# A streaming-encoder block on one core: c spread by a load, the opening's first step by parts, and gate B applied inside attention

## The chip, the core and the metric

The kernel runs on one core of a Trainium2 chip. A core has TensorE (PE in the profile, with its weight loads as PEld), VectorE (DVE), ScalarE (ACT), GpSimd (POOL) and SyncE (SP); each works through its own instructions in order, and semaphores hold an instruction until what it needs is there. DMAs are issued by SP and ACT as items of their instruction queues. Matrix products go from SBUF to PSUM, which has eight banks of 128 x 512 fp32. The metric is the device time of one execution in microseconds (us), lower is better.

## What is computed

One layer of an encoder block for 1024 tokens of width 1024 (16 heads of 64, FFN width 2816), in fp32:

```python
mod = silu(c) @ ada_w + ada_b
sh1, sc1, g1, sh2, sc2, g2 = split(mod, 6)
h = rmsnorm(x, ln1_g) * (1 + sc1) + sh1
q, k, v, cb, cc, cx, ga, gb = split(h @ w_in)          # conv B, C, x; gates A, B
q, k = rmsnorm(q), rmsnorm(k)                          # per head
y_a = stick_breaking_attention(q, k, v)                # strictly causal, scan over the keys
y_b = cb * causal_dwconv(cc * cx, conv_w)
merged = sigmoid(ga) * (y_a @ w_branch_a) + sigmoid(gb) * (y_b @ w_branch_b)
x = x + g1 * (merged @ w_out)
h = rmsnorm(x, ln2_g) * (1 + sc2) + sh2
x = x + g2 * ((silu(h @ w_ffn_gate) * (h @ w_ffn_up)) @ w_ffn_down)
```

## The kernel before

**Products.** Each fp32 operand is split in a high part (rounded to fp32r, tiles named `hi`, `whi`, `hh`, `yh`) and a low rest (`lo`, `wlo`, `hl`, `yl`); a product is three passes, hi by hi, hi by lo and lo by hi, added up in one PSUM bank. For most splits ACT makes the high part and DVE the rest.

**Stages.** (1) The opening, (2) a second pass over w_kv and the k part, (3) the gates and convolution inputs (Strassen products), which store sigmoid(ga) and sigmoid(gb) to DRAM as `d_sga` and `d_sgb`, (4) attention, (5) the merge, (6) the output projection, (7) the FFN. A planner (a simulated timeline) orders instructions on the engines by their priority; the opening's order is kept as written, and in attention so are all PE instructions and attention's own on DVE.

**The opening** multiplies x, not yet normed, so that PE can start early. `cab` is silu(c) on all partitions: one row of c (`crow`, 4 KB) is loaded on the ACT queue, two products with a row of ones (L326) spread it over 128 partitions, and two Silus (L327) write it. `mod_dot` (L237, DVE) takes a strip of the ada weights (`ld<-ada`) times `cab` and sums it into one column; `scale_sum` makes of it `a1`, the scale of 128 features. `raw_hi` (L263, ACT) and `raw_lo` (L267, DVE) write hi and lo of x times a1; `split_hi` (L217) and `split_lo` (L222) split the weights. `real` (L294) adds, for each of eight steps k over the features, three passes for each of NR = 6 token blocks into six banks `psr`: in every step MC = 2 blocks first, then the other four. `warm` runs NW = 4 fp32 products of nothing of use (two passes each, L329) ahead of the first real one. Behind the eight steps `tail` does two more token blocks with the same operands; `square` (L252, ACT) has meanwhile summed the squares of x (`ld<-x`), `finish_raw` scales the finished blocks and empties their banks (L310 on ACT for even ones, L308 on DVE for odd ones), and `bcast` (L258, PE) writes the norm factors into banks thus emptied (`rsp`), for the products that follow. The loads stand on SP in the order ada, x, w_kv, ada, x and so on.

**Attention** (L870 to L1100) goes head by head: scores on PE (L900, L901), exponentials on ACT (L902), a scan on DVE (L910), transposes on PE (L924), their splits (L927 on ACT, L928 on DVE) and products with v. The scores leave PE time; `fillers()` yields other products into it: first C times B (`cb_w`), then W_b (L1000 to L1002, through `mm_ch`), for 16 pairs of an output block m and a token half n. ACT copies each finished W_b product out of its bank (`mb`, L1042), and SP stores it to DRAM (`d_mb`).

**The merge** (L1129 to L1153) forms for each of the same 16 pairs the W_a product (24 passes), and joins the branches: SP loads `sa` (sigmoid of gate A, tag "sgi", two buffers, L1139), `mb` (three buffers, L1141) and `sb` (sigmoid of gate B, tag "yr", two buffers, L1143); POOL multiplies mb by sb (L1144); DVE multiplies the product by sa (L1147, this empties the PSUM bank) and adds mb (L1148); ACT and DVE split the sum (L1152, L1153). Near the end `preload_wo` (L1107, one raw buffer) loads the first weights of the output projection and splits them (L1111 on ACT, L1112 on DVE).

Of the kernel before, what the change touches and what calls it, by code (L numbers as in the profile page):

```python
# [9 lines left out]
F32 = mybir.dt.float32  # L10
F32R = mybir.dt.float32r
AF = mybir.ActivationFunctionType
ALU = mybir.AluOpType
# [4 lines left out]
P = 128  # L18
T = 1024
D = 1024  # L20
# [10 lines left out]
def block_kernel(tc, x, x_t, cols, ada_1, ada_2, ada_row, w_q, w_kv, w_cg, w_a, w_b, w_o, w_g, w_u, w_d, out):  # L31
    nc = tc.nc
# [7 lines left out]
    def nm(s):  # L40
        uid[0] += 1
        return f"{s}_{uid[0]}"
# [31 lines left out]
    d_sgb = drp.tile([KT, P, T], F32, name="d_sgb")  # L74
# [7 lines left out]
    d_h = [drp.tile([P, 4, 512], F32, name=f"d_h{e}") for e in range(2)]  # L82
# [5 lines left out]
    mk = const.tile([P, D], F32, name="mk")  # L88
# [12 lines left out]
    nhalf = const.tile([P, 8], F32, name="nhalf")  # L101
    nc.vector.memset(nhalf, -0.5)
    cst = const.tile([P, 98], F32, name="cst")
    nc.scalar.dma_start(cst, cols)
    ct, ln1, ln2 = cst[:, 0:8], cst[:, 8:16], cst[:, 16:24]
    acol = cst[:, 24:56].rearrange("p (m k) -> p m k", m=4)
    cw = cst[:, 56:80].rearrange("p (k t) -> p k t", k=8)
    qgc, kgc = cst[:, 80:81], cst[:, 81:82]
    gcol = cst[:, 82:98].rearrange("p (m k) -> p m k", m=2)
    nc.vector.tensor_scalar(out=qgc, in0=qgc, scalar1=0.125, scalar2=None, op0=ALU.mult)  # L110
    mod = const.tile([P, 4, 8], F32, name="mod")
    const.tile([P, PADL // 4], F32, name="padl")
    st.enter_context(tc.tile_pool(name="padr", bufs=1, side="right", reuse_waits="tile")).tile(
# [30 lines left out]
    def ps_pj():  # L144
        return pps.tile([P, 512], F32, tag="pj", bufs=6, name=nm("pj"))
# [26 lines left out]
    sp = s1.enter_context(tc.tile_pool(name="start", bufs=1, reuse_waits="tile"))  # L172
# [4 lines left out]
        return xts[:, k, ns]  # L177

    cab = sp.tile([P, D], F32, name="cab")
    crow = sp.tile([1, D], F32, name="crow")  # L180
    nc.scalar.dma_start(crow, ada_row[0:1, :])
    rs = sp.tile([P, T], F32, name="rs")
    hh = [big() for n in range(2)]
    hl = [big() for n in range(2)]
# [14 lines left out]
        ads[m, k] = load_ring(ada_1[k][:, m])  # L199

    wq = []
    NLD, MC, NW, KB = 5, 2, 4, 2

    def load_wq(qt):
        wp, bufs = wps
# [9 lines left out]
    def split_hi(k):  # L215
        cs = slice(k % 2 * 512, k % 2 * 512 + 512)
        nc.scalar.activation(wq[k // 2][0][:, cs], wraw[k // 2][:, cs], AF.Copy)  # L217

    def split_lo(k):
        cs = slice(k % 2 * 512, k % 2 * 512 + 512)  # L220
        hi, lo = wq[k // 2]
        nc.vector.tensor_tensor(out=lo[:, cs], in0=wraw[k // 2][:, cs], in1=hi[:, cs].bitcast(F32), op=ALU.subtract)  # L222
# [17 lines left out]
    def scale_sum(k):  # L240
        nc.vector.scalar_tensor_tensor(out=a1[:, k:k + 1], in0=mod_dot(1, k), scalar=acp[:, k:k + 1],
                                       in1=ln1[:, k:k + 1], op0=ALU.add, op1=ALU.mult)
# [53 lines left out]
    def real(pss, k, ts, w):  # L296
        for parts in ((0,), (1,), (2,)):
            for i in ts:
                mm_tok(pss[i], i, w, k, k + 1, parts)
# [21 lines left out]
    load_ada(1, 3)  # L321
    load_x(3)
    warm = ps_tr()
    for e in range(2):
        t = ps_pj()
        nc.tensor.matmul(t, mk[0:1, D - P:], crow[:, e * 512:e * 512 + 512], start=True, stop=True)  # L326
        nc.scalar.activation(cab[:, e * 512:e * 512 + 512], t, AF.Silu)  # L327
    for e in range(NW):
        nc.tensor.matmul(warm, ident, mk[:, 512:], start=True, stop=True)  # L329
    scale_sum(0)  # L330
    raw_hi(0)
    split_hi(0)
    scale_sum(1)
    split_lo(0)
    raw_lo(0)
    split_hi(1)
    NR = 6
    psr = [ps_pj() for i in range(NR)] + [ps_tr() for i in range(8 - NR)]
    for k in range(KT):
        real(psr, k, range(MC), wq)  # L340
        if k + 1 < KT:
            raw_hi(k + 1)
            split_lo(k + 1)
        if k + 2 < KT:
            scale_sum(k + 2)
            split_hi(k + 2)
        if k + 1 < KT:
            raw_lo(k + 1)
        real(psr, k, range(MC, NR), wq)
        if k + 4 < KT:  # L350
            load_ada(1, k + 4)
            load_x(k + 4)
        if k % 2 == 0 and k < 6:
            load_wq(k // 2 + 2)
        if k > 2:
            load_xq(k - 3)
        if k > 3:
            square(k - 4)
# [199 lines left out]
    for cc in (1, 2):  # L558
        w = wq[8:] if cc == 1 else [load_w(w_kv[3, j]) for j in range(4)]
        for i_, i in enumerate(range(8) if cc == 1 else (4, 5, 6, 7, 0, 1, 2, 3)):  # L560
# [12 lines left out]
            ps = ps_pj()  # L573
# [227 lines left out]
    sg_.close()  # L801
    ftx.close()
    split_at[:] = [gw]
    for e in range(2):
        nc.sync.dma_start((hh, hl)[e][1][:, :4].bitcast(F32), d_h[e])
    psA.close()


# [195 lines left out]
    def fillers():  # L1004
        cb_w = {}
        for m, n in [(m + d, n) for m in range(0, KT, 2) for n in range(2) for d in range(2)]:
            if n == 0:
                cb_w[m] = load_ch(w_cg[0, m])
            w = cb_w[m]
            y = fp.tile([P, 512], F32, tag="st", bufs=3, name=nm("cy"))  # L1010
            nc.sync.dma_start(y, d_y[m, :, n * 512:(n + 1) * 512])
            ps = ps_f()
            for kk in range(0, KT, KQ):
                if kk:
                    yield 0.65 * KQ
                mm_ch(ps, w, hh[n], hl[n], kk, kk + KQ)
            nc.vector.tensor_tensor(out=y, in0=ps, in1=y, op=ALU.mult)
            yh = fq.tile([P, 512], F32R, tag="ybh", bufs=2, name=nm("ybh"))
            yl = fq.tile([P, 512], F32R, tag="ybl", bufs=2, name=nm("ybl"))
            nc.scalar.activation(yh, y, AF.Copy)  # L1020
            nc.vector.tensor_tensor(out=yl, in0=y, in1=yh.bitcast(F32), op=ALU.subtract)
            nc.sync.dma_start(d_yb[0][n][:, m, :], yh.bitcast(F32))
            nc.sync.dma_start(d_yb[1][n][:, m, :], yl.bitcast(F32))
            yield 0.65 * KQ
        yh, yl = [], []
        for n in range(2):
            yh.append(big())
            yl.append(big())
            for k in range(0, KT, 2):
                nc.sync.dma_start(yh[n][:, k:k + 2].bitcast(F32), d_yb[0][n][:, k:k + 2])  # L1030
                nc.sync.dma_start(yl[n][:, k:k + 2].bitcast(F32), d_yb[1][n][:, k:k + 2])
        wb = {}
        for m, n in [(0, 0), (1, 0), (0, 1), (1, 1)] + [(m, n) for m in range(2, KT) for n in range(2)]:
            if n == 0:
                wb[m] = load_ch(w_b[m])
            ps = ps_f()
            for kk in range(0, KT, KQ):
                if kk:
                    yield 0.65 * KQ
                mm_ch(ps, wb[m], yh[n], yl[n], kk, kk + KQ)  # L1040
            mb = fp.tile([P, 512], F32, tag="st", bufs=3, name=nm("mb"))
            nc.scalar.activation(mb, ps, AF.Copy)  # L1042
            nc.sync.dma_start(d_mb[m, :, n * 512:(n + 1) * 512], mb)
            yield 0.65 * KQ

# [16 lines left out]
    with tc.high_priority():  # L1062
        for j in range(HEAD):
            next(fl)
            if j == 1:
                vl = load_vlast(0)
                turn_vlast(0, vl)
                att_load(0)
                load_v(0, 1)
                load_v(0, 0)  # L1070
    at_ = attention()
    flush, nfl = [0], 0
    pe, mine = len(nc.cur_bb.bb.instructions), set()
# [58 lines left out]
    for m, n in [(0, 0), (1, 0), (0, 1), (1, 1)] + [(m, n) for m in range(2, KT) for n in range(2)]:  # L1132
        if (m, n) == (KT - 2, 0):
            with tc.issue_after(last_m.ins):
                preload_wo()
        if n == 0:
            wa[m] = load_ch(w_a[m])
        sa = fp.tile([P, 512], F32, tag="sgi", bufs=2, name=nm("sgi"))
        nc.sync.dma_start(sa, d_sga[m, :, n * 512:(n + 1) * 512])  # L1139
        mb = fp.tile([P, 512], F32, tag="st", bufs=3, name=nm("mb"))  # L1140
        nc.sync.dma_start(mb, d_mb[m, :, n * 512:(n + 1) * 512])  # L1141
        sb = fp.tile([P, 512], F32, tag="yr", bufs=2, name=nm("sgb"))
        nc.sync.dma_start(sb, d_sgb[m, :, n * 512:(n + 1) * 512])  # L1143
        nc.gpsimd.tensor_tensor(out=mb, in0=mb, in1=sb, op=ALU.mult)  # L1144
        ps = ps_f()
        mm_ch(ps, wa[m], yah[n], yal[n])
        last_m = nc.vector.tensor_tensor(out=sa, in0=ps, in1=sa, op=ALU.mult)  # L1147
        nc.vector.tensor_tensor(out=sa, in0=sa, in1=mb, op=ALU.add)  # L1148
        if m == 0:
            mh[n] = big()  # L1150
            mlo[n] = big()
        nc.scalar.activation(mh[n][:, m, :], sa, AF.Copy)  # L1152
        nc.vector.tensor_tensor(out=mlo[n][:, m, :], in0=sa, in1=mh[n][:, m, :].bitcast(F32), op=ALU.subtract)  # L1153
# [110 lines left out]
    for ch in range(2):  # L1264
# [21 lines left out]
        for i in (0, 4, 1, 2, 3, 5, 6, 7) if ch else range(8):  # L1286
# [8 lines left out]
            ps = bank()  # L1295
# [396 lines left out]
```

## Time and profile before

| what | us |
|---|---|
| three runs, median (lowest, highest) | 1832.03 (1830.80, 1834.08) |
| the profiled execution | 1830.19 |
| its span in the profile | 1828.4 |
| PE busy in the span | 1795.6 |
| DVE, ACT, POOL busy | 1360.4, 815.2, 388.9 |
| 16 products mb by sb on POOL, together (mean of one) | 21.6 (1.353) |

Rows of the timeline give start (us from the start of the span), duration (with xN the duration of N in a run of them), engine, line, operation, output<-input, shapes, and in brackets how long the engine stood idle before it and what ended that. Rows of the waits of PE give total us, times, and the longest. Groups by line end with busy us and the mean ns of one, then the idle time before them. Rows of windows are a stretch of the span with the busy time of PE, PEld, DVE, ACT and POOL, the granted clock of PE (1.00 is full), the busy share of the DMA engines and their GB/s. Rows on DMA give the size and the time from issue to landing. Passes overlap in PE, so the distance of two starts tells more than one's duration.

### The profile page before, as it was taken

How to read it: one execution, taken by the hardware profiler on the slowest of the kernel's cores; microseconds unless marked ns; L12 is line 12 of the kernel's file. 1: busy time of each engine (PE TensorE's matmuls, PEld its weight loads, DVE VectorE, ACT ScalarE, POOL GpSimd, SP SyncE). 2: the span in 40 equal slices, each digit the busy share in tenths (PEclk: the TensorE clock that was granted, in tenths of full speed). 3: DMA queues.
4: the chain of work that ended last, by engine and by line, in shares of the span. 5: the costliest groups of instructions: out<-in, count | busy, mean ns of one | idle time of the engine just before them, and what ended most of it. 6: DMA issues, size and time to landing. Idle time of an engine off the chain costs nothing. (4 is left out here: it accounts for less than half of the span.)

```text
span 1828.4 us, 24603 instructions
## 1 busy us (share of the span) xinstructions
PE 1795.6 (98%) x8635; PEld 1490.9 (82%) x8635; DVE 1360.4 (74%) x1964; ACT 815.2 (45%) x1527; POOL 388.9 (21%) x293
## 2 busy tenths in 40 slices
PE   8999999999999899999999989999999999999999
PEld 6888877888778788888888868877888888878887
DVE  5876586778895699998886544689977878644766
ACT  5434364333433476777675221664444344322321
POOL 0024334633232000000000210114534544200000
PEclk9999999999999999999999999999999999999999
DMA  9479644223684977696544656424543444299776
GB/s 365 155 240 383 237 176 141 84 98 112 236 291 161 265 204 184 194 330 153 146 114 132 201 173 221 136 87 162 195 148 140 149 164 160 105 361 326 278 230 219
DMA packets 164960, 359.05 MB, mean 196 GB/s; under 512 B 15507, under 2 KB 60891, under 8 KB 163686
## 3 DMA queue, kind: packets, MB, share of 16 engines
q1 hardware_dynamic: 128300, 289.65, 48.2%
q10 hardware_dynamic: 35530, 64.16, 9.8%
q0 software_dynamic: 1008, 3.67, 0.5%
q8 instruction: 69, 1.13, 0.3%
q14 instruction: 53, 0.43, 0.1%
HBM read 246.80 MB, written 110.66 MB: 196 GB/s over the span
## 5 line engine op out<-in xcount | busy, mean ns | idle before, releaser
L910 DVE TENSOR_TENSOR_SCAN pt<-pt,mk 128x128 f32<-128x128 f32 (+7 forms) x128 | 172.5, 1347 | 3.7 <-ACT pt L902 3.7
L133 PE MATMUL e<-big,whi 128*128 128x512 f32 x352 | 137.3, 390 | 2.8 <-ACT c L1420 1.4
L135 PE MATMUL e<-big,wlo 128*128 128x512 f32 x352 | 137.0, 389 | 0.0
L134 PE MATMUL e<-big,whi 128*128 128x512 f32 x352 | 137.0, 389 | 0.0
L294 PE MATMUL pj<-whi,big 128*128 128x512 f32 x448 | 132.9, 393 | 0.0
L138 DVE TENSOR_TENSOR c<-e,c 128x512 f32<-128x512 f32 x138 | 92.8, 686 | 49.7 <-PE e L135 48.6
L133 PE MATMUL pj<-big,whi 128*128 128x512 f32 x320 | 125.3, 392 | 1.8 <-DVE c L138 1.8
L1144 POOL TENSOR_TENSOR mb<-mb,sgb 128x512 f32<-128x512 f32 x16 | 21.6, 1353 | 494.3 <-DMA mb<-d_mb 454.5
L135 PE MATMUL pj<-big,wlo 128*128 128x512 f32 x320 | 124.8, 390 | 0.0
L134 PE MATMUL pj<-big,whi 128*128 128x512 f32 x320 | 124.6, 389 | 0.0
L1520 PE MATMUL e<-whi,f 128*128 128x512 f32 (+1 forms) x319 | 121.8, 382 | 1.4 <-DMA f<-d_f 1.4
L1521 PE MATMUL e<-wlo,f 128*128 128x512 f32 (+1 forms) x319 | 121.8, 382 | 0.0
L1522 PE MATMUL e<-whi,f 128*128 128x512 f32 (+1 forms) x319 | 121.6, 382 | 0.0
L138 DVE TENSOR_TENSOR c<-pj,c 128x512 f32<-128x512 f32 x140 | 93.2, 682 | 35.9 <-PE pj L135 35.0
L902 ACT ACTIVATE pt<-z,rq 128x512 f32<-128x512 f32 (+1 forms) x192 | 105.2, 577 | 23.5 <-PE z L901 22.8
L138 POOL TENSOR_TENSOR ws<-raw,raw 128x512 f32<-128x512 f32 x40 | 55.0, 1374 | 280.4 <-DMA raw<-w_cg 134.0
L928 DVE TENSOR_TENSOR atl<-tr,ath 128x512 fp32r<-128x512 f32 (+1 forms) x192 | 103.3, 550 | 14.9 <-ACT ath L927 12.8
L1000 PE MATMUL pj<-big,whi 128*128 128x512 f32 x256 | 114.0, 445 | 0.0
L927 ACT ACTIVATE ath<-tr 128x512 fp32r<-128x512 f32 (+1 forms) x192 | 93.0, 488 | 30.0 <-PE tr L924 29.1
L134 PE MATMUL e<-rl,whi 128*128 128x512 f32 x264 | 102.8, 389 | 1.5 <-DVE rl L138 1.5
L133 PE MATMUL e<-rh,whi 128*128 128x512 f32 x264 | 102.7, 389 | 0.0
L135 PE MATMUL e<-rh,wlo 128*128 128x512 f32 x264 | 102.7, 389 | 0.0
(272 smaller groups left out, 4872.4 us busy)
## 6 DMA issues: line engine op xcount, KB each, us to landing
f<-d_f SPq DMA_DIRECT2D x77, 512.0 KB, 5.0
d_f<-fs SPq DMA_DIRECT2D x70, 512.0 KB, 3.5
raw<-w_cg SPq DMA_DIRECT2D x40, 512.0 KB, 3.3
raw<-w_u SPq DMA_DIRECT2D x26, 512.0 KB, 3.4
raw<-w_g SPq DMA_DIRECT2D x25, 512.0 KB, 3.6
raw<-w_kv SPq DMA_DIRECT2D x20, 512.0 KB, 4.7
ad<-ada ACTq DMA_DIRECT2D x19, 512.0 KB, 4.5
ld<-ada SPq DMA_DIRECT2D x16, 512.0 KB, 4.2
```

Of the source, the lines that this page charges most:

```text
L133: nc.tensor.matmul(ps, wh[:, k, :], fh[:, k, :], start=(k == 0), stop=False)
L134: nc.tensor.matmul(ps, wh[:, k, :], fl[:, k, :], start=False, stop=False)
L135: nc.tensor.matmul(ps, wl[:, k, :], fh[:, k, :], start=False, stop=(k == 3))
L138: eng.tensor_tensor(out=out, in0=a, in1=b, op=op)
L294: nc.tensor.matmul(ps, a, b, start=(k == 0 and q == 0), stop=(k == KT - 1 and q == 2))
L902: nc.scalar.activation(pt[:, off + s0:off + s0 + m], z[:, :m], AF.Sigmoid, scale=rq[:, 1, i, h:h + 1])
L910: nc.vector.tensor_tensor_scan(out=pt[:, rev], data0=pt[:, rev], data1=mk[:, rev], initial=1.0, op0=ALU.mult, op1=ALU.max)
L928: nc.vector.tensor_tensor(out=tl[:, :nb, c0:c0 + P], in0=src, in1=th[:, :nb, c0:c0 + P].bitcast(F32), op=ALU.subtract)
L1000: nc.tensor.matmul(ps, wh, rh_, start=(k == 0), stop=False)
L1520: nc.tensor.matmul(o, sh, w[0][:, c], start=(j == 0), stop=False)
L1521: nc.tensor.matmul(o, sh, w[1][:, c], start=False, stop=False)
L1522: nc.tensor.matmul(o, sl, w[0][:, c], start=False, stop=(j == NJ - 1))
```

## The change

Two places are edited.

**Opening.** `crow`, its two products and the two Silus of 512 columns are gone: `cab` is loaded by one DMA of the row of c to all 128 partitions (512 KB) and goes through one Silu in place. This load stands first in the ACT queue, and `cst` (the small columns) behind it. NW is 3, and these products need only `mk` and the identity. The high part of the first weights is made ahead of big on ACT, its rest ahead of the second dot on DVE. The first step of `real` takes all six blocks by parts (six hi by hi, six with wlo, six with the low part of x).

**Gate B.** Inside attention the finished W_b product is multiplied by `sb` on DVE straight out of PSUM, where ACT copied it before; `sb` is loaded there, into the two "sgi" buffers, two of them ahead of the first W_b product. The merge has no load of `sb` and no product on POOL; its `mb` holds the gated value. Beside this, the two loads of `d_h` are written at the head of attention, no longer at the end of the gates stage.

```diff
-    nc.scalar.dma_start(cst, cols)
...
     cab = sp.tile([P, D], F32, name="cab")
-    crow = sp.tile([1, D], F32, name="crow")
-    nc.scalar.dma_start(crow, ada_row[0:1, :])
+    nc.scalar.dma_start(cab, ada_row[0:1, :].broadcast_to([P, D]))
+    nc.scalar.dma_start(cst, cols)
+    nc.vector.tensor_scalar(out=qgc, in0=qgc, scalar1=0.125, scalar2=None, op0=ALU.mult)
...
-    NLD, MC, NW, KB = 5, 2, 4, 2
+    NLD, MC, NW, KB = 5, 2, 3, 2
...
     warm = ps_tr()
-    for e in range(2):
-        t = ps_pj()
-        nc.tensor.matmul(t, mk[0:1, D - P:], crow[:, e * 512:e * 512 + 512], start=True, stop=True)
-        nc.scalar.activation(cab[:, e * 512:e * 512 + 512], t, AF.Silu)
     for e in range(NW):
         nc.tensor.matmul(warm, ident, mk[:, 512:], start=True, stop=True)
+    nc.scalar.activation(cab, cab, AF.Silu)
+    split_hi(0)
     scale_sum(0)
     raw_hi(0)
-    split_hi(0)
+    split_lo(0)
     scale_sum(1)
-    split_lo(0)
     raw_lo(0)
     split_hi(1)
...
     for k in range(KT):
-        real(psr, k, range(MC), wq)
+        mc = MC if k else NR
+        real(psr, k, range(mc), wq)
...
-        real(psr, k, range(MC, NR), wq)
+        real(psr, k, range(mc, NR), wq)
...
-    for e in range(2):
-        nc.sync.dma_start((hh, hl)[e][1][:, :4].bitcast(F32), d_h[e])
...
+        def load_sb(m, n):
+            sb = fp.tile([P, 512], F32, tag="sgi", bufs=2, name=nm("sgi"))
+            nc.sync.dma_start(sb, d_sgb[m, :, n * 512:(n + 1) * 512])
+            return sb
+
+        sbs = [load_sb(m, 0) for m in range(2)]
...
+            sb = sbs.pop(0) if sbs else load_sb(m, n)
...
-            nc.scalar.activation(mb, ps, AF.Copy)
+            nc.vector.tensor_tensor(out=mb, in0=ps, in1=sb, op=ALU.mult)
...
+                for e in range(2):
+                    nc.sync.dma_start((hh, hl)[e][1][:, :4].bitcast(F32), d_h[e])
...
-        sb = fp.tile([P, 512], F32, tag="yr", bufs=2, name=nm("sgb"))
-        nc.sync.dma_start(sb, d_sgb[m, :, n * 512:(n + 1) * 512])
-        nc.gpsimd.tensor_tensor(out=mb, in0=mb, in1=sb, op=ALU.mult)
```

What this does to the order of instructions is shown at three places; numbers behind names tell tiles of one kind apart. First PE at its start, before the change (`crow` the row of c, `mk`/`dm` the warming operands, `big` the high and low parts of x, `pj` the six banks):

```order
L326 MATMUL pj_173<-crow,mk 128x512
L326 MATMUL pj_176<-crow,mk 128x512
L329 MATMUL tr_172<-mk,dm 128x512 x4
L294 MATMUL pj_196<-whi_157,big_144 128x512
L294 MATMUL pj_197<-whi_157,big_144 128x512
L294 MATMUL pj_196<-wlo_158,big_144 128x512
L294 MATMUL pj_197<-wlo_158,big_144 128x512
L294 MATMUL pj_196<-whi_157,big_146 128x512
```

and with it:

```order
L324 MATMUL tr_171<-mk,dm 128x512 x3
L293 MATMUL pj_189<-whi_156,big_143 128x512
L293 MATMUL pj_190<-whi_156,big_143 128x512
L293 MATMUL pj_191<-whi_156,big_143 128x512
L293 MATMUL pj_192<-whi_156,big_143 128x512
L293 MATMUL pj_193<-whi_156,big_144 128x512
L293 MATMUL pj_194<-whi_156,big_144 128x512
L293 MATMUL pj_189<-wlo_157,big_143 128x512
```

The warming products are first and one fewer, and the first pass with wlo comes seventh, where it came third. Next SP near the end of the merge, before:

```order
L1141 DMA mb_10619<-d_mb 128x512
L1139 DMA sgi_10581<-d_sga 128x512
L1143 DMA sgb_10703<-d_sgb 128x512
L1107 DMA raw_10555<-w_o 128x1024
L1141 DMA mb_10665<-d_mb 128x512
L1139 DMA sgi_10617<-d_sga 128x512
L1107 DMA raw_10565<-w_o 128x512
```

and with the change:

```order
L1145 DMA mb_10605<-d_mb 128x512
L1143 DMA sgi_10570<-d_sga 128x512
L1111 DMA raw_10544<-w_o 128x1024
L1145 DMA mb_10648<-d_mb 128x512
L1143 DMA sgi_10603<-d_sga 128x512
L1111 DMA raw_10554<-w_o 128x512
```

The load of gate B that stood ahead of the second w_o load is gone, and nothing else stands in its place. Last DVE in attention with the change, around the fifth gated product (the scan of L910 is `L905 SCALAR_TENSOR_TENSOR` here, the split of the transposes L923):

```order
L905 SCALAR_TENSOR_TENSOR pt_5185<-pt_5185,mk 128x896
L941 TENSOR_TENSOR oy_8397<-o_8387,otmp_8396 64x256
L923 TENSOR_TENSOR atl_8369<-tr_8415,ath_8368 128x4x128
L923 TENSOR_TENSOR atl_8381<-tr_8425,ath_8380 128x2x128
L905 SCALAR_TENSOR_TENSOR pt_5186<-pt_5186,mk 128x1024
L1044 TENSOR_TENSOR mb_8459<-pj_8317,sgi_8315 128x512
L923 TENSOR_TENSOR atl_8448<-tr_8449,ath_8447 128x4x128
```

The product (L1044) stands between a scan and a split of transposes that PE's later products wait for; before, DVE had nothing there.

More of the change, by code (lines that the diff above doesn't have):

```diff
@@ L109, in block_kernel @@
     gcol = cst[:, 82:98].rearrange("p (m k) -> p m k", m=2)
-    nc.vector.tensor_scalar(out=qgc, in0=qgc, scalar1=0.125, scalar2=None, op0=ALU.mult)
     mod = const.tile([P, 4, 8], F32, name="mod")
```

## The prediction

> **What bounds the kernel now.** I read the page's first part, then the waits of PE, then windows by stage, then the timelines of the places that the change touches.
>
> ```profile
> PE 1795.6 (98%) x8635; PEld 1490.9 (82%) x8635; DVE 1360.4 (74%) x1964; ACT 815.2 (45%) x1527; POOL 388.9 (21%) x293
> ...
> PE pj L1000 <- DVE sgi L1147: 7.3, 3, 6.3
> PE pj L326 <- DMA crow<-ada_row: 5.5, 1, 5.5
> ...
> 25.00:50.00 25.00, 25.00 (x112) 20.70 (x111) 14.72 (x28) 15.97 (x29) 2.06 (x2) 1.00 0.92 340
> ...
> 625.00:800.00 175.00, 172.98 (x1075) 149.72 (x1074) 168.10 (x236) 121.58 (x277) 0.00 (x0) 1.00 0.77 214
> 800.00:1000.00 200.00, 198.95 (x1215) 173.31 (x1214) 173.15 (x241) 138.23 (x312) 0.00 (x0) 1.00 0.57 160
> ...
> 1075.00:1100.00 25.00, 18.60 (x75) 15.00 (x76) 11.34 (x16) 5.83 (x10) 3.34 (x2) 0.86 0.60 211
> 1100.00:1125.00 25.00, 25.00 (x112) 20.71 (x111) 14.06 (x22) 3.20 (x6) 0.00 (x0) 1.00 0.68 231
> ```
>
> PE is busy 98% of the span, so time can only come from its few gaps, and the two largest waits are the two places that the change edits: the end of the merge stage (7.3 us) and the start (5.5 us). The windows (columns: us, busy PE, PEld, DVE, ACT, POOL, granted clock, DMA share, GB/s) show that PE is full behind both places (25.00 of 25), so what is won there is kept. In attention PE is nearly full, too, and DVE is the next engine: 173.15 of 200.
>
> **The opening.** Its timeline, with the issues and landings of the first stretch:
>
> ```profile
> 2.12 0.29 POOL L90 TENSOR_SCALAR_AFFINE_SELECT mk<-mk 128x128 f32<-128x128 f32 x1
> ...
> 9.17 6.47 PE L329 MATMUL tr<-mk,dm 128*128 128x512 f32 x8
> 9.90 1.23 DVE L237 CUSTOM_DVE_ANT_0 ld<-ld,cab 128x1024 f32<-128x1024 f32 x1 [4.04 <-ACT cab L327]
> 11.43 1.33 ACT L263 ACTIVATE big<-xts,a 128x512 fp32r<-128x512 f32 x2 [1.55 <-DVE a L241]
> 12.67 1.13 ACT L217 ACTIVATE whi<-raw 128x512 fp32r<-128x512 f32 x2
> 15.08 1.02 PE L294 MATMUL pj<-whi,big 128*128 128x512 f32 x2
> ...
> 43.63 1.06 ACT L252 ACTIVATE ld<-ld 128x1024 f32<-128x1024 f32 x1 [2.48 <-DMA ld<-x]
> 47.77 0.67 ACT L310 ACTIVATE vs<-pj,rs_r 128x512 f32<-128x512 f32 x1
> 48.13 0.39 PE L294 MATMUL tr<-whi,big 128*128 128x512 f32 x1
> 48.51 2.06 DVE L308 TENSOR_SCALAR vs<-pj,rs_r 128x512 f32<-128x512 f32 x3
> 50.85 1.95 PE L258 MATMUL pj<-dm,rs_r 128*128 128x128 f32 x16
> 52.55 0.48 PE L294 MATMUL tr<-whi,big 128*128 128x512 f32 x1
> ...
> raw<-w_kv SPq DMA_DIRECT2D x1, 512.0 KB, 6.3
> ...
> 6.00:8.00 2.00, 2.00 (x3) 0.66 (x2) 0.00 (x0) 0.43 (x1) 0.00 (x0) 1.00 1.03 421
> ...
> 44.00:46.00 2.00, 2.00 (x10) 1.65 (x10) 0.00 (x0) 1.86 (x4) 0.00 (x0) 1.00 1.03 412
> ```
>
> Before, the chain to the first real product is: c lands (the 5.5 of PE's waits), one-row products, Silu, DVE's dot of c with ada from 9.90, then big and whi on ACT, and products from 15.08, behind 8 passes of warming.
>
> Removed: the one-row products and one of the two Silus. Added: a load of 512 KB (c to all partitions, 524 KB in the rows' thousands), ahead of everything that the ACT queue loads. At the 421 GB/s of window 6 to 8 it takes 524/421 = 1.25 us of a DMA that is full there, and all loads behind it land that much later. I put c and the first ada strip at about 6.65 (5.5 + 1.2; an estimate), Silu of 1024 columns at 1.06 (the square at 43.63 has that size), so the dot at 7.75 instead of 9.90. But the first weights landed at 1.63 + 6.3 = 7.93 and now land at about 9.2. The hi half (0.6) is first in ACT's order, then big (0.65): the first product at about 10.4, 4.7 earlier. The three warming products are six passes of 0.86 (6.47 for 8, the last of them faster) from 2.5, when mk is there (2.12 + 0.29), to 7.7; then PE waits 2.65 us. What such a wait does to the clock, a like place in attention shows:
>
> ```profile
> 610.48 0.30 PE L900 MATMUL z<-skh,sqt 128*128 128x128 f32 x1 [1.56 <-DMA skh<-d_k]
> 611.75 0.30 PE L901 MATMUL z<-skl,sqt 128*128 128x128 f32 x1 [0.98 <-DMA skl<-d_k]
> ...
> 612.00:614.00 2.00, 2.00 (x8) 1.73 (x8) 0.42 (x1) 0.64 (x2) 0.00 (x0) 0.53 1.05 357
> ```
>
> Two waits of 2.5 us together, and the clock is 0.53. The eight steps take 33.05 us now (15.08 to 48.13): from 10.4 they end at 43.45, with 0.45 for the second ada strip, late too, at 43.9 if the clock stays up. I let the first eight products cost twice instead (8 x 0.2 = 1.6, which covers the 0.45): 45.0. That is 3.1 to 4.2 us ahead of 48.13.
>
> Of this most does not pass, I think. PE next has the tail of two tokens (48.13 to 50.85, 2.7 us) and then `bcast` (L258), whose two banks come free only when two tokens of v have left them (L310 on ACT, the first L308 on DVE); these wait for the sums of squares of x, whose last loads stand behind all the others. Before, the two moves were done at 47.77 + 0.67 = 48.44 and 48.51 + 0.69 = 49.2, 1.65 us ahead of `bcast`: PE came last. Now PE would be there 3 us earlier, and the moves come last. DMA is full around x's loads (1.03 from 44 to 46; ACT waits 2.48 for x at 43.63), so the last x lands later by the added 1.25, less what earlier consumers fill of the 8% left free (0.92 of the first 50 us), of which I take at most 0.55: 0.7 to 1.25 later. The moves end at 49.1 to 49.7 and 49.9 to 50.5; the second half of `bcast` (0.85) follows the second: done at 50.75 to 51.4, against 52.55. **Opening: -1.5**, bounds +1.2 (everything follows the later x) and -4.0 (x arrives in time). The first step part by part moves no work; it only puts the products with wlo and the lo halves of x later, where they are ready.
>
> [...]
>
> **The merge.** SP is one queue; what stands in it behind a waiting issue waits too.
>
> ```profile
> 1068.83 0.42 SPq L1139 DMA_DIRECT2D sgi<-d_sga  x1
> 1075.00 0.32 SPq L1143 DMA_DIRECT2D sgb<-d_sgb  x1
> 1075.41 0.38 SPq L1107 DMA_DIRECT2D raw<-w_o  x1
> ...
> 1067.99 1.29 DVE L1112 TENSOR_TENSOR wlo<-raw,whi 128x512 fp32r<-128x512 f32 x2
> 1073.69 1.28 POOL L1144 TENSOR_TENSOR mb<-mb,sgb 128x512 f32<-128x512 f32 x1 [5.75 <-DMA mb<-d_mb]
> 1079.26 1.15 ACT L1111 ACTIVATE whi<-raw 128x512 fp32r<-128x512 f32 x2 [8.11 <-DMA raw<-w_o]
> 1079.92 2.36 DVE L1112 TENSOR_TENSOR wlo<-raw,whi 128x512 fp32r<-128x512 f32 x2 [4.99 <-ACT whi L1111]
> 1086.37 0.68 DVE L1147 TENSOR_TENSOR sgi<-pj,sgi 128x512 f32<-128x512 f32 x1
> 1088.91 0.69 DVE L1153 TENSOR_TENSOR big<-sgi,big 128x512 fp32r<-128x512 f32 x1 [0.69 <-ACT big L1152]
> ...
> sgi<-d_sga SPq DMA_DIRECT2D x16, 256.0 KB, 3.8
> ...
> 1087.11 0.80 PE L1000 MATMUL pj<-ya,whi 128*128 128x512 f32 x1 [6.32 <-DVE sgi L1147]
> 1089.83 0.47 PE L1000 MATMUL pj<-ya,whi 128*128 128x512 f32 x1
> ```
>
> The sgb load at 1075.00 needs a buffer that POOL's product frees at 1074.97; the second w_o load stands right behind it, though its own buffer is free from 1069.28. It lands at 1079.26 (3.85 after its issue), and DVE, in order, stands 4.99 us before the split of w_o while the products that free PE's banks wait behind it: PE stops 6.32 us. With no sgb load the queue goes on behind the sga load at 1068.83: w_o at about 1069.3, landed at 1073.1, before DVE needs it. The sga loads keep their two buffers: from L1147 to the buffer's release 3.2 us (1086.37 to 1088.91 + 0.69), landing 3.8, and 1.3 for the issues between make 8.3 (an estimate), of the 10.8 that two products take (48 passes at 0.225; 25.00/112 in the last window is 0.223), so they do not replace the wait. Recovered: the 7.3 us of waits (three of them), and the half clock behind the long one: 1087.11 to 1089.83 is 2.72 us for six passes that otherwise take 1.35: 1.4. **Merge: -8.6**; bounds -8.9 (with what else DVE waits) and about -3 (below).
>
> [...]
>
> **Attention.** ACT loses 16 copies, DVE gains 16 products; its like is L1147 in the merge (0.68, PSUM by SBUF), and ahead of it in DVE's order stand scans:
>
> ```profile
> L910 DVE TENSOR_TENSOR_SCAN pt<-pt,mk 128x1024 f32<-128x1024 f32 x8 | 18.2, 2280 | 0.0
> L1042 ACT ACTIVATE mb<-pj 128x512 f32<-128x512 f32 x15 | 9.0, 597 | 0.6 <-PE pj L1002 0.2
> ```
>
> 16 x 0.60 to 0.68 = 9.6 to 10.9 us on DVE, in a window with 200 - 173.15 = 26.85 idle; DVE goes from 87 to 92%. The stretch before it has DVE at 168.10 of 175 (96%) and PE idle 2.02 of 175, against 1.05 of 200 here. Taking half of that difference (1.15% - 0.53% = 0.6% of 200 = 1.3 us) as the price: **+0.6**, bounds 0 and +1.3. Behind a product on DVE stand scans and atl splits; PE's transposes wait for them. ACT's 9.6 us less gains nothing: it is 69% busy (138.23 of 200) and no wait of PE names it. The 16 sgb loads (256 KB) go to a stretch with DMA share 0.57 and stand behind the d_mb store on SP; PE takes 12.5 us a product there, so a landing of 4 us is hidden. If that cover went, PE's bank would wait, which the rival below prices. The d_h loads keep their place on SP: nothing. Some rows of the first FFN pairs swap on DVE and ACT: 0, with 1.5 either way.
>
> **Sum**: -1.5 - 8.6 + 0.6 = -9.5, so the profiled execution of 1830.19 becomes 1820.7. The median of the runs is 1.84 above that execution: **1822** (its own range 1818 to 1826).
>
> **Rivals.** *x does not bound the opening* (0.13): the free share of DMA swallows the added load, the gain is 3.1 to 4.0, and the time 1820. For: DVE's and ACT's moves would start sooner; against: DMA at 1.03 until 46. *The merge's stall stays in part* (0.12): the w_o load stays behind sga or mb in the queue and DVE stops again; then only the port's 1.07 and some two us come back, 3 in all: 1830.19 - 1.5 - 3 + 0.6 + 1.84 = 1828. For: sga has only two buffers; against: 2.5 us of slack. *c lands late* (0.07): the broadcast takes longer than its bytes, and the opening gains nothing: 1823.5. *DVE becomes the bound of attention, slower* (0.06): a product in DVE's order stands waiting for PE's last pass while scans behind it are ready. Free are 26.85/16 = 1.68 us per product; above that PE waits, and from (26.85 + 10.1)/16 = 2.3 the whole is slower than before. At 0.6 and one scan of the longest kind (2.28) it is 2.9 a product: 46.4 - 26.85 = 19.5 us, and 1830.19 - 10.1 + 19.5 + 1.84 = 1841. For: DVE's queue is in order; against: 13% idle and products placed behind scans. Another 0.02 I cannot name.
>
> **How the numbers follow.** The forecast has 0.60. About 0.2% (3.7 us) can be told from no change: faster is below 1828.4. Forecast, first and third rival: 0.80, and a little of the second: 0.82 faster; most of the second 0.10 the same; the last and what is not named 0.08. The range, 1816 to 1830, holds the cases with gain and leaves out the slower one.
>
> **What would show it.** Right: a wait of PE on L1147's successor gone or under 1 us in the merge, no clock below 1.00 there, w_o issued near 1069 less what came before; first real product near 10.4 and the first product behind `bcast` near 51; DVE in attention 5% busier, PE idle there under 2.5 us in 200. Wrong: a new wait on sga or mb in the merge; `bcast` near 49 or at 52.5; PE waits on pt or atl of 10 us and more in attention.

## The result, and the profile after

| | before | changed |
|---|---|---|
| five runs each, median us (lowest, highest) | 1834.08 (1830.80, 1834.25) | 1824.70 (1821.87, 1826.85) |
| ratio of the runs, 95% interval | | 0.9954 (0.9940 to 0.9969) |
| the profiled execution, us | 1830.19 | 1824.70 |
| its span, us | 1828.4 | 1822.9 |

The change makes the kernel 9.4 us faster by the medians, 5.5 us between the two profiled executions; a second measurement, below, gave 0.9971 (0.9959 to 0.9984). The page's first part for the changed kernel:

```profile
PE 1794.7 (98%) x8629; PEld 1492.0 (82%) x8629; DVE 1362.9 (75%) x1980; ACT 809.6 (44%) x1510; POOL 367.4 (20%) x277
```

and its waits of PE (total us, times, longest):

```profile
PE tr L919 <- DVE pt L905: 4.8, 8, 1.6
PE e L131 <- ACT c L1421: 3.8, 1, 3.8
PE pj L293 <- ACT big L262: 3.1, 1, 3.1
PE tr L324 <- POOL mk L90: 2.5, 1, 2.5
PE pj L133 <- DVE wlo L136: 2.0, 1, 2.0
...
PE pj L995 <- DVE mb L1044: 1.2, 1, 1.2
```

The 7.3 us of waits on L1147 are gone, and so are the 5.5 us on `crow`. In their place stand new ones: 2.5 and 3.1 us in the opening (on `mk` and on `big`), 3.8 us on ACT in the FFN, 1.2 us on the new DVE product, and 4.8 for 3.8 us on the scans. Since PE is busy nearly all the time, the question where time went is best put to PE: I set the start of the same pass in two traces side by side, each counted from the start of its span, and look where their distance changes. The table has these changes in us (negative is gained against the first trace of before), for the change and for the runs of the next section.

| trace | opening (to 55) | 55 to 605 | 605 to 625 | attention (to 1006) | merge (to 1095) | first FFN pairs (1240 to 1270) | whole span |
|---|---|---|---|---|---|---|---|
| the change | -2.9 | +2.4 | -0.5 | +2.3 | -9.5 | +3.2 | -5.5 |
| change_again | -3.0 | -0.8 | -0.2 | +1.0 | -9.5 | +2.3 | -10.1 |
| before_again | -0.3 | +0.6 | -0.1 | -0.1 | -1.6 | 0.0 | -1.4 |
| opening_alone | -3.0 | 0.0 | -0.4 | -0.1 | -1.3 | +3.3 | -1.9 |
| gate_alone | -0.6 | +3.3 | -0.3 | +1.7 | -9.5 | 0.0 | -6.0 |
| ffn_order_kept | -2.9 | +3.9 | +1.0 | +2.6 | -9.5 | 0.0 | -5.2 |
| w_o_on_act | 0.0 | -0.4 | -0.4 | -0.5 | -4.8 | +1.4 | -4.7 |
| gate_b_not_loaded | -0.1 | +3.0 | -0.1 | -0.4 | -9.5 | +0.6 | -6.4 |
| five_warm | -2.8 | -0.3 | -0.3 | +1.4 | -9.5 | +0.6 | -11.0 |
| dummy_load | -1.5 | +3.4 | +2.3 | +2.3 | -9.5 | +1.0 | -3.0 |
| copy_and_dve | -2.5 | +3.2 | -0.1 | +1.1 | -9.5 | +1.0 | -7.1 |
| copy_and_pool | -2.3 | -0.8 | -0.4 | +4.5 | -9.5 | +0.6 | -8.7 |
| all_three | -2.9 | +3.1 | +1.1 | +1.4 | -9.5 | +1.0 | -6.4 |

Four terms belong to the change: opening, attention, merge, FFN. The columns 55 to 605 and 605 to 625 vary between traces of one program (the two rows of the change: +2.4 and -0.8). The other columns vary less, but not by nothing: with the merge of before, before_again and opening_alone are 1.6 and 1.3 us shorter there than the first trace, so the change's gain in the merge is 7.9 to 9.5 us, by the trace that it is counted against.

**Opening after.** Its timeline:

```profile
10.58 2.92 PE L293 MATMUL pj<-whi,big 128*128 128x512 f32 x6 [3.06 <-ACT big L262]
...
44.84 0.39 PE L293 MATMUL tr<-whi,big 128*128 128x512 f32 x1
...
45.55 1.06 ACT L251 ACTIVATE ld<-ld 128x1024 f32<-128x1024 f32 x1
...
47.13 0.67 ACT L309 ACTIVATE vs<-pj,rs_r 128x512 f32<-128x512 f32 x1
47.85 2.05 PE L257 MATMUL pj<-dm,rs_r 128*128 128x128 f32 x16
49.66 0.48 PE L293 MATMUL tr<-whi,big 128*128 128x512 f32 x1
```

and the windows from 10 to 14 us (columns as in the prediction; the clock is the third number from the end):

```profile
10.00:12.00 2.00, 1.42 (x3) 1.16 (x4) 1.96 (x5) 1.66 (x3) 0.00 (x0) 0.59 1.03 348
12.00:14.00 2.00, 2.00 (x7) 1.54 (x6) 2.00 (x5) 1.33 (x2) 0.00 (x0) 0.56 1.00 385
```

The first product starts at 10.58 (before 15.08), behind 3.06 us of idle time, at half clock; the tail starts at 44.84 (48.13), and the first product behind `bcast` at 49.66 (52.55).

**Merge after.** SP, ACT and DVE around the second w_o load:

```profile
1066.13 0.33 SPq L1111 DMA_DIRECT2D raw<-w_o  x1
1069.43 1.15 ACT L1115 ACTIVATE whi<-raw 128x512 fp32r<-128x512 f32 x2 [1.47 <-DMA raw<-w_o]
1070.26 1.29 DVE L1116 TENSOR_TENSOR wlo<-raw,whi 128x512 fp32r<-128x512 f32 x2
```

and the windows of the stage:

```profile
1045.00:1070.00 25.00, 25.00 (x112) 20.71 (x111) 12.96 (x20) 5.63 (x11) 0.00 (x0) 1.00 0.41 134
1070.00:1095.00 25.00, 25.00 (x112) 20.71 (x111) 13.67 (x22) 5.43 (x10) 0.00 (x0) 1.00 0.63 201
```

The load is issued at 1066.13, right behind the first pair of splits; the next pair runs at 1070.26, in 1.29 us where it took 2.36. PE has no gap in 50 us, and the clock stays at 1.00.

**FFN after.** The timeline at the wait of 3.8 us:

```profile
1245.71 3.46 DVE L1183 TENSOR_TENSOR wlo<-raw,whi 128x512 fp32r<-128x512 f32 x2
1249.09 0.68 DVE L136 TENSOR_TENSOR fs<-wt,fs 128x512 fp32r<-128x512 f32 x1
1250.30 0.68 DVE L136 TENSOR_TENSOR fs<-wt,fs 128x512 fp32r<-128x512 f32 x1
1250.41 0.60 ACT L1421 ACTIVATE c<-e 128x512 f32<-128x512 f32 x1 [2.35 <-DVE fs L136]
1251.06 0.79 PE L131 MATMUL e<-big,whi 128*128 128x512 f32 x1 [3.79 <-ACT c L1421]
```

and a window behind it:

```profile
1249.00:1256.00 7.00, 4.94 (x12) 3.88 (x13) 6.97 (x13) 3.49 (x6) 0.00 (x0) 0.53 0.89 332
```

The timeline of the same place before, where DVE and ACT had their rows in another order:

```profile
1254.13 0.50 PE L133 MATMUL e<-big,whi 128*128 128x512 f32 x1 [1.33 <-DVE c L138]
...
1255.67 0.68 DVE L1182 TENSOR_TENSOR wlo<-raw,whi 128x512 fp32r<-128x512 f32 x1
...
1258.56 0.50 PE L133 MATMUL e<-big,whi 128*128 128x512 f32 x1 [1.42 <-ACT c L1420]
```

In the changed order two splits (3.46 us beside POOL) stand ahead of DVE's `fs` rows; ACT's copy of `c`, which empties a bank, starts behind these, and PE stops 3.79 us where it stopped 1.33 and 1.42. The clock is at 0.53 in the window behind it.

### The profile page after: what moved, and what is told of

Same layout as the page of the kernel before. It is cut to its first block, busy times and chain, and to the rows that moved or that the text cites. A ratio compares the mean times of both kernels' runs of the same rounds, so it can differ in the third digit from the quotient of the medians.

```text
span 1822.9 us, 24550 instructions
## 1 busy us (share of the span) xinstructions
PE 1794.7 (98%) x8629; PEld 1492.0 (82%) x8629; DVE 1362.9 (75%) x1980; ACT 809.6 (44%) x1510; POOL 367.4 (20%) x277
## 4 chain that ended last, share of the span: by engine, by line
PE 83%; DVE 8%; DMA 5%; issue 2%; ACT 1%; POOL 0%; SPq 0%; ACTq 0%; DVEq 0%; POOLq 0%
PE e L131 7%; PE e L133 7%; PE e L132 7%; PE pj L293 7%; PE pj L131 5%; PE pj L133 5%; PE pj L132 5%; PE pj L995 4%; PE pj L997 4%; PE pj L996 4%; PE e L1521 4%; PE e L1523 4%; PE e L1522 4%; PE tr L919 3%; PE o L935 2%
## 5 line engine op out<-in xcount | busy, mean ns | idle before, releaser
L905 DVE TENSOR_TENSOR_SCAN pt<-pt,mk 128x128 f32<-128x128 f32 (+7 forms) x128 | 172.6, 1348 | 3.2 <-ACT pt L897 3.2
L923 DVE TENSOR_TENSOR atl<-tr,ath 128x512 fp32r<-128x512 f32 (+1 forms) x192 | 103.1, 550 | 9.2 <-ACT ath L922 7.2
```

What stands on the lines that cost most here:

```text
L905: nc.vector.tensor_tensor_scan(out=pt[:, rev], data0=pt[:, rev], data1=mk[:, rev], initial=1.0, op0=ALU.mult, op1=ALU.max)
L923: nc.vector.tensor_tensor(out=tl[:, :nb, c0:c0 + P], in0=src, in1=th[:, :nb, c0:c0 + P].bitcast(F32), op=ALU.subtract)
```

## The experiments

All runs are beside runs of before on the same chip; the trace of each gives its row in the table above.

**opening_alone** and **gate_alone**: the kernel before with one half of the diff each, word for word as in the section on the change (the d_h loads in neither).

> The kernel before with the opening's edits alone (loaded c, three warming products, first step by parts); gate B stays in the merge. In this kernel DVE's and ACT's rows of the first FFN pairs stand in the changed order. Theory (the opening gives about 2.9 us at the first product behind bcast, and its changed planner times cost about 3.2 us in the first FFN pairs): the two cancel, the whole is within 2 us of before, a wait of PE on ACT's copy of 3 us and more with a half clock stands in the first FFN pairs, and the merge keeps its wait of about 6 us on DVE. Rival (the FFN loss came from elsewhere, from the gate B edit or by chance): about 3 us faster than before and no such wait in the FFN.

Measured: 1830.59 us against 1829.40, ratio 1.0012 (1.0001 to 1.0023); within 2 us, as the theory has it. The first product behind `bcast` comes 3.0 us earlier, the FFN loses 3.3, and the timeline of PE has the wait again:

```profile
1254.53 0.79 PE L131 MATMUL e<-big,whi 128*128 128x512 f32 x1 [3.75 <-ACT c L1417]
```

> The kernel before with the gate B edit alone (product on DVE inside attention, no gate B load and no POOL product in the merge); opening and FFN stand in the order of before. Theory: attention costs about 2 us, the merge gives 9.5 (its waits of 7.3, the half clock, and small ones), together 7 to 7.5 us faster than before, so faster than the full change has been less its opening, and no wait above 2 us in the first FFN pairs. Rival (gate B edit pays the FFN loss): 4 us faster.

Measured: 1823.65 against 1829.40, 0.9968 (0.9957 to 0.9979). Attention +1.7, merge -9.5, FFN 0.0: the theory's terms. The sum, 5.8 us by the medians, lies between the theory's 7 to 7.5 and the rival's 4; in this trace 55 to 605 lost 3.3 us. Together with opening_alone this makes the FFN loss the opening's doing. It isn't by anything that the opening computes: the planner orders rows by simulated times, and other times in the opening changed its choices 1200 us later (how it came to them was not followed). With the issue of one small load moved it chooses as before:

**ffn_order_kept**

```diff
-    nc.scalar.dma_start(cst, cols)
+    nc.sync.dma_start(cst, cols)
```

> The changed kernel with one difference in the text: the small load of columns (cst, 49 KB) is issued by SP ahead of its first strip and not by ACT behind c. With it DVE's and ACT's rows of the first FFN pairs stand as before the change; the rest of the order is the changed kernel's. Theory (the FFN loss of 3.2 us is the order of these rows): 3 us faster than the changed kernel, 11 to 12 us faster than before, opening unchanged within 0.5 us. Rival (that loss is chance of the clock): no difference from the changed kernel, about 9 us faster than before.

Measured: 1821.82 against 1829.40, 0.9963 (0.9950 to 0.9976). The FFN's loss is 0.0, with the two old waits back (1.30 and 1.40), as the theory has it. In the runs it is not clear: 0.9963 lies between the change's 0.9954 and 0.9971. On the chip of the second of these it is 2.9 us below the change by the medians (1824.69, below), with intervals that overlap; in this trace the stages that vary lost 5 us. The expected 11 to 12 us were missed. The order is not all of the FFN column either: the traces with the order of before, or all of it but two rows, have 0.0 to +1.4 there, and those with the changed order +2.3 to +3.3.

**w_o_on_act**: before, with the early w_o loads on ACT's queue.

```diff
-            nc.sync.dma_start(raw[:, :nk * 512], w_o[0, j, :, :nk * 512])
+            nc.scalar.dma_start(raw[:, :nk * 512], w_o[0, j, :, :nk * 512])
```

> The kernel before with the three early w_o loads near the end of the merge issued on ACT's queue and not on SP's; gate B's loads and POOL products stay. Theory (the wait of 6.3 us comes from the w_o load standing behind gate B's load in the SP queue): that wait goes, and the merge is 6 to 8.6 us shorter, so is the whole. Rival (POOL's products, and DVE's splits slowed beside them, hold the merge): the wait of PE on L1147 stays at 4 us or more, the whole moves by less than 3 us.

Measured: 1826.66 against 1829.40, 0.9988 (0.9978 to 0.9997). The waits of PE at the end of the merge:

```profile
PE pj L1000 <- ACT whi L1111: 1.4, 1, 1.4
PE pj L1000 <- DVE sgi L1147: 0.5, 1, 0.5
```

The wait of 6.3 us is gone though gate B's loads and POOL's products are all there. From 1070 to 1095 PE gains 6.4 us; 1.6 are lost again in the stretch before, so 4.8 in all, less than the 6 to 8.6 expected. That left open whether the other half is POOL's.

**gate_b_not_loaded**: before, the loads of gate B in the merge left out, POOL's products kept.

```diff
-        sb = fp.tile([P, 512], F32, tag="yr", bufs=2, name=nm("sgb"))
-        nc.sync.dma_start(sb, d_sgb[m, :, n * 512:(n + 1) * 512])
-        nc.gpsimd.tensor_tensor(out=mb, in0=mb, in1=sb, op=ALU.mult)
+        nc.gpsimd.tensor_tensor(out=mb, in0=mb, in1=mb, op=ALU.mult)
```

> The kernel before without the 16 loads of gate B in the merge; POOL's 16 products stay and multiply mb by itself. The output leaves out gate B. PE's, DVE's and ACT's rows stand as before; on SP nothing but the 16 loads is missing. With the early w_o loads on ACT's queue the merge became 4.8 us shorter, with the whole change 9.5. Theory (the loads in the SP queue make the whole of it, and moving w_o to ACT's queue only put new waits there): the merge is 8.5 to 9.5 us shorter. Rival (POOL's products hold the rest, by their length or by slowing DVE beside them): 4 to 7 us shorter, with waits of PE on L1147 of 2 us and more left.

Measured (one execution): 1823.84 us, and the merge as in the change, -9.5, with POOL at work in it, by its windows:

```profile
1045.00:1070.00 25.00, 25.00 (x112) 20.71 (x111) 13.31 (x20) 5.69 (x9) 4.17 (x4) 1.00 0.38 127
1070.00:1095.00 25.00, 25.00 (x112) 20.71 (x111) 13.93 (x20) 5.99 (x10) 2.38 (x2) 1.00 0.60 208
```

So the whole gain of the merge is that 16 loads left the SP queue; once they are gone, POOL's products cost nothing there. The two splits of the second w_o load still take 2.13 us beside one of them in this trace (1.29 in the change), but nothing waits for that.

**five_warm** and **dummy_load** (both on the run with the FFN order kept):

```diff
-    NLD, MC, NW, KB = 5, 2, 3, 2
+    NLD, MC, NW, KB = 5, 2, 5, 2
```

```diff
     split_hi(1)
+    dum = sp.tile([P, D], F32, name="dum")
+    nc.scalar.dma_start(dum, ada_row[0:1, :].broadcast_to([P, D]))
     NR = 6
```

> The run with the FFN order kept, with five warming products in place of three. PE's idle time of 2.5 to 3 us ahead of the first real product should shrink to under 2, the clock should stay at 1.00 there, and the eight steps should end 1 to 1.5 us earlier (43.4 in place of 44.8). Theory (bcast waits for the two moves that empty its banks, and these for x): the first product behind bcast stays within 0.4 us of 49.6, no gain in the whole. Rival (PE is still what comes last): it comes 1 us or more earlier.

Measured: 1821.95 against 1829.38, 0.9964 (0.9949 to 0.9978). The timeline of PE at the first product and at `bcast`:

```profile
10.35 1.65 PE L293 MATMUL pj<-whi,big 128*128 128x512 f32 x6 [0.75 <-ACT big L262]
...
47.95 2.05 PE L257 MATMUL pj<-dm,rs_r 128*128 128x128 f32 x16 [1.42 <-ACT vs L309]
```

With 0.75 us of idle time the clock stays up (1.00 from 12 to 28 us; 0.93 there in ffn_order_kept, behind 2.47 us), and PE is 1 us further at the tail (4.5 us ahead of before, not 3.5); it spends this waiting at `bcast`, which starts at 47.95, no earlier than the change's 47.85. The whole is as fast as ffn_order_kept (0.9963): no gain, as expected.

> The run with the FFN order kept, with one more load of 512 KB that nothing uses (the row of c to all partitions again, into a tile of its own), issued by ACT behind the first step's operands. Two DVE rows of the first FFN pairs swap. Theory (in the changed kernel DMA moves 410 to 420 GB/s without a gap up to the last x, so that each load ahead of it delays it): the sums of squares end 1.25 us later, and so does bcast: first product behind it near 50.9. Rival (DMA has slack, as the earlier x of the changed kernel suggests): both stay within 0.4 us.

Measured (one execution): 1827.2 us. Its timeline at ACT's last square and `bcast`:

```profile
46.90 1.06 ACT L251 ACTIVATE ld<-ld 128x1024 f32<-128x1024 f32 x1
...
49.20 2.05 PE L257 MATMUL pj<-dm,rs_r 128*128 128x128 f32 x16 [0.15 <-ACT vs L309]
```

Both are 1.35 us later than in the change (45.55, 47.85): the theory. PE, too, came later to the tail here, by 1.6 us against ffn_order_kept (granted clock 0.85 from 12 to 28 us, not 0.93), but that is not what moves the squares: in copy_and_dve and copy_and_pool it came 1.0 and 1.2 us later, and their last squares began at 45.59 and 45.67. In the changed kernel the x loads do set when `bcast` runs, and another 512 KB put it off by 1.35 us (1.25 expected).

**copy_and_dve** and **copy_and_pool** (on the run with the FFN order kept): where the product with gate B is made inside attention.

```diff
-            nc.vector.tensor_tensor(out=mb, in0=ps, in1=sb, op=ALU.mult)
+            nc.scalar.activation(mb, ps, AF.Copy)
+            nc.vector.tensor_tensor(out=mb, in0=mb, in1=sb, op=ALU.mult)
```

copy_and_pool has the second line with `nc.gpsimd` for `nc.vector`.

> The run with the FFN order kept, and in it the finished W_b product is first copied out of PSUM by ACT, as before the change; DVE then multiplies the copy by gate B. DVE's work is the same as in the change (16 products of 0.68), but PE's bank is free after the copy. Theory (the price of gate B in attention, 1.7 to 2.6 us so far, is DVE's work in its order: scans come later, and PE's transposes wait for them): attention's start to the first W_a products still costs 1 to 2.6 us against before; only the 1.2 us wait of PE on DVE's last product goes. Rival (PE waits for its banks): the price falls under 0.6.

Measured: 1823.13 against 1829.38, 0.9969 (0.9954 to 0.9985). Attention costs 1.1 us, and the wait of 1.2 us on DVE's last product is gone. The change itself costs 1.0 to 2.6 in six traces, so the rest of the price stays, as the theory says; whether the copy saves anything reliably, these traces do not tell.

> The run with the FFN order kept, with ACT's copy as before the change, and POOL, which has nothing else to do in attention, multiplies the copy by gate B there. Theory (DVE's added work is the price): the price of 1.7 to 2.6 us in attention goes to about 0, the whole is 2 us faster than the run with the FFN order kept, since 16 products of 1.3 us are small beside 400 us. [...]

Measured: 1825.72 against 1829.38, 0.9981 (0.9969 to 0.9994). Attention costs 4.5 us, where the theory has about 0. The groups by line of DVE's scans, its splits of the transposes (`atl`) and of weights (`wlo`), and of POOL's products, from 800 to 1000 us:

```profile
L905 DVE TENSOR_TENSOR_SCAN pt<-pt,mk 128x384 f32<-128x384 f32 (+7 forms) x62 | 89.9, 1449 | 0.0
L923 DVE TENSOR_TENSOR atl<-tr,ath 128x512 fp32r<-128x512 f32 (+2 forms) x96 | 51.8, 550 | 9.9 <-ACT ath L922 8.8
...
L136 DVE TENSOR_TENSOR wlo<-raw,whi 128x512 fp32r<-128x512 f32 x15 | 12.9, 858 | 0.7 <-ACT whi L516 0.7
...
L1045 POOL TENSOR_TENSOR mb<-mb,sgi 128x512 f32<-128x512 f32 x15 | 22.3, 1484 | 404.5 <-ACT mb L1044 404.5
```

and the same DVE groups, with the new product, in the change:

```profile
L905 DVE TENSOR_TENSOR_SCAN pt<-pt,mk 128x256 f32<-128x256 f32 (+7 forms) x63 | 85.9, 1363 | 0.0
L923 DVE TENSOR_TENSOR atl<-tr,ath 128x512 fp32r<-128x512 f32 (+2 forms) x98 | 53.1, 553 | 6.3 <-ACT ath L922 5.4
...
L136 DVE TENSOR_TENSOR wlo<-raw,whi 128x512 fp32r<-128x512 f32 x16 | 10.9, 682 | 0.3 <-ACT whi L516 0.3
L1044 DVE TENSOR_TENSOR mb<-pj,sgi 128x512 f32<-128x512 f32 x15 | 10.2, 679 | 1.9 <-PE pj L997 1.7
```

With POOL's products in the stretch the mean scan takes 1.45 us for 1.36 and a weight split 0.86 for 0.68; the `atl` splits, which read PSUM and one SBUF tile, stay at 0.55. So in this stretch the scans and weight splits, which have both inputs in SBUF, took longer and the `atl` splits did not (0.550 us for 0.553); no run takes apart why. The change's product, which reads PSUM and one SBUF tile as the `atl` splits do, takes 0.68. DVE is no busier in all than in the change (177.65 of 200 us, for 180.07); single scans come later, and from 800 us on PE waits 3.2 us for scans, where it waited 1.6. Of the three places tried, the engine with nothing to do was the dearest.

**before_again, change_again, all_three**: the two kernels once more, and the change with cst on SP, five warming products and ACT's copy.

> The kernel before, once more, for the trace alone. In the gates stage (538 to 552 us) five of nine other traces lost 2.3 to 3.9 us against the first trace of before, four lost nothing, with the same program on every engine up to there. Theory (chance, the same for all kernels): this trace may show either, but nothing between; a loss comes with a wait of PE on wlo of about 2 us and a half clock. Rival (something of the gate B edit): no loss here.

Measured (one execution): 1828.76 us. It has the wait of PE on wlo (2.1 us, 1.4 in the first trace) and lost 0.8 us from 538 to 552, about that difference. So there is something between, against the theory's first half; but gate_b_not_loaded, without the gate B edit in attention, lost 2.9 there, and three traces with it lost nothing: the edit is neither needed for the loss nor enough for it. Six of nine traces with the edit have it and one of five without, too few to rule out that the edit makes it likelier.

> The changed kernel, once more, beside the next run on the same chip. Theory: 6 to 9 us faster than before, with the FFN loss of 3 us (wait of PE on ACT's copy of c near 1250) again in the trace. Rival (that wait was chance): no such wait.

Measured: 1824.69 against 1829.62, 0.9971 (0.9959 to 0.9984): 5 us by the medians, less than the 6 to 9 expected. The wait in the FFN is there again (3.75 us); its trace has no loss from 55 to 605.

> The changed kernel with cst issued by SP (FFN rows as before the change), five warming products, and in attention ACT's copy ahead of DVE's product. Theory: against the changed kernel 3 us from the FFN and 1 us from attention, none from the opening: 3 to 5 us faster than the changed kernel, 10 to 13 faster than before. Rival (the stages that differ by chance hide it, or the copy costs what it gives): within 2 us of the changed kernel.

Measured: 1823.67, on the same chip as the 1824.69 of change_again; 0.9960 (0.9946 to 0.9973) against before. That is the rival: within 2 us. The FFN gained 1.3 us, not 3, attention nothing. No version tried is clearly faster than the change.

## Why the prediction was right or wrong, point by point

The range of the forecast, 1822 (1816 to 1830), holds the 1824.7. That the sum came so near is in part luck: two terms gained 2.3 us more than forecast, two lost 4.9 us more. (By its own terms the prediction's time is 1822.5, and that of its third rival 1824.0; the half us is rounding, and nothing hangs on it.)

- **Opening, -1.5: direction right, size half.** The steps up to the bound were right: first product 10.4 (10.58), half clock behind the idle time, end of the steps 45.0 (44.84), and the moves last at `bcast` (five_warm). The step that failed is "the last x lands later by the added 1.25, less ...": the last square began 0.65 us *earlier* (45.55, shown above) than before:

```profile
46.20 1.06 ACT L252 ACTIVATE ld<-ld 128x1024 f32<-128x1024 f32 x1
```

  Some of the 0.65 is chance: it began at 45.51 to 46.20 in five traces with the old opening, at 45.41 to 45.67 in eight with the new one and no further load. But it came no later. The prediction had taken the room from the DMA share, 8% free. There was more: the windows from 28 to 44 us, before and after (last two numbers: share and GB/s), move 16% more bytes in the same time, for a share of 1.03 in place of 0.96.

```profile
28.00:44.00 16.00, 16.00 (x72) 13.27 (x71) 9.49 (x17) 9.97 (x19) 1.04 (x1) 1.00 0.96 357
```

```profile
28.00:44.00 16.00, 16.00 (x73) 13.23 (x72) 7.77 (x15) 9.90 (x18) 1.04 (x1) 1.00 1.03 414
```

  The loads of before were held back by their buffers, which consumers free, and these run earlier now (the w_kv read of 29.26 is issued at 27.54). That this is why is argued from the issues, not shown by a run of its own; that DMA is now the bound is shown by dummy_load. The first rival had the half of it: the added load was swallowed, and the gain of 2.9 is near its 3.1 to 4.0; but x still bounds. By the prediction's own signs this term was wrong: the first product behind `bcast` came at 49.66, not near 51, and "near 49" stood among the signs of being wrong.
- **Merge, -8.6: right.** -8.9 from 1070 to 1095 and 0.6 ahead of it against the first trace of before; against the other two with its merge 7.9 and 8.2 in all. The mechanism, the gate B load ahead of w_o in the SP queue, is shown from two sides, by moving w_o and by leaving out the loads. The 1.07 us that two splits lost beside POOL did come back (1.29 for 2.36). Without gate B's loads that is on no path: gate_b_not_loaded keeps POOL and gains as much. With them it seems to be inside the wait: in before_again the same two splits took 1.30 us, and PE waited 5.0 us, not 6.3:

```profile
PE pj L1000 <- DVE sgi L1147: 5.0, 1, 5.0
```

  No run shows the port to which the second rival puts its 1.07 us; the runs show the times of the splits alone, 2.36 us for two beside POOL's product and 1.29 in the change.

- **Attention, +0.6 (0 to 1.3): too small.** 1.0 to 2.6 in six traces. DVE became busier by 6.9 us in the window from 800 to 1000 (180.07 of 200, for 173.15); 9.6 to 10.9 were forecast. The price had been taken from how a stretch with DVE at 96% differs from this one, in PE's idle share; it left out that PE also waits for the bank that DVE's product now frees (1.2 us on L1044, at the end, where DVE's splits stand ahead), and scans that come later cost 0.8 more from 800 on (1.6 us of waits for 0.8).
- **FFN, 0 with 1.5 either way: wrong.** It is +2.3 to +3.3, wherever the rows stand in the changed order. Half clock behind the wait is part of it: 5.2 us of it in the change (0.53 in the window shown above), 3.4 in change_again, by its passes (starts 0.43 us apart, then 0.23). The order of a few rows on DVE and ACT looked harmless because PE's own order was the same; what counted, as the timelines have it, was which row frees PE's bank, and what stands ahead of it.
- The d_h loads: nothing, as forecast (no trace shows a difference that would be theirs; not tried alone).

Opening 1.4 and merge 0.9 more, attention 1.7 and FFN 3.2 less than forecast: -9.5 - 2.3 + 4.9 = -6.9; the rest of the difference to -5.5 is the stages that vary. The median of the runs was 9.4 us lower in one measurement and 4.9 in the other, and the forecast of 10 is at the upper end.

## What to carry to other kernels

Look at what stands in a DMA queue behind a load that waits for a buffer: here a load for one engine held a weight load for another, and taking it out of the queue gave 8 to 9.5 us where the product it fed cost nothing. A share of DMA time near 1 is no proof that DMA is full: at 0.96 there was room for 16% more bytes here. Compare the GB/s with the best that the same trace reaches. And where a planner orders instructions by simulated times, any edit can reorder a stage far away: read the order around the rows that free PSUM banks, and price a swap there.

## What the runs showed of the hardware

In the traces of before and the change half clock came in pieces of 3.41 or 6.83 us (the one that runs past the end of the span left out), and each began in a wait of PE or up to 0.9 us behind one. Before, 3.41 us of it began at 612.1 (waits of 1.56 and 0.98 us) and 6.83 at 1083.2 (6.32); in the change, 3.41 at 10.4 (3.06), 542.8 (1.99) and 611.1 (1.27 and 0.75), and 6.83 at 1249.4 (3.79). Ahead of the first real product, idle times of 2.47 (ffn_order_kept) and 3.06 us (the change) stood before a granted clock of 0.93 and 0.94 from 12 to 28 us, 3.25 (dummy_load) before 0.85, and 0.75 (five_warm) before 1.00. In the gates stage of the change the wait was 2.0 us (clock 0.72 in the window around it), and one of 1.4 at the same place before had no half clock behind it (1.00 from 538 to 552); in before_again one of 2.1 came with a loss of 0.8 us. PE's timeline at that place in the change:

```profile
541.96 0.50 PE L133 MATMUL pj<-ft,wlo 128*128 128x512 f32 x1 [1.99 <-DVE wlo L136]
```

and the window around it:

```profile
541.00:547.00 6.00, 5.04 (x15) 3.98 (x16) 4.91 (x11) 3.15 (x6) 0.00 (x0) 0.72 0.87 273
```

What decides whether half clock follows such a wait, no run here shows. Against the first trace of before, where PE waited 1.4 us there, the wait cost 0.8 us in before_again and 2.3 to 3.9 us in seven other traces: a good part of why single traces of one program differ by up to 5 us.
